# A hybrid Fourier/Hyena encoder layer: another order in the first half of its Fourier stage, xg stored by halves, a table loaded later

## The chip, the cores and the metric

The kernel runs on one core of a Trainium2 chip. The metric is the device time of one execution in microseconds, as the median of several runs; three runs of the kernel before took 2352.02, 2353.79 and 2360.07 us. One more execution was taken with the hardware profiler, and all views of the trace come from it.

## What is computed

One encoder layer is applied to two inputs of 1024 x 1024, here called batch 0 (the prompt) and batch 1 (the sample). Cut to what matters:

```
xn = rmsnorm(x, g_pre)
p  = xn @ w_in                       # 8 sections of 1024 columns
fv, fg, hv, hg, mg = split(p)
fz  = real(fft over the sequence and over groups of 256 channels of fv)
y_f = (fz * silu(fg)) @ w_fourier_out
v, x1, x2 = split(short_conv(hv))
z = v
for n, gate in enumerate((x1, x2)):
    z = gate * long_conv(z, filter[n], d[n])     # FFT convolution, length 2048
y_h = (z * silu(hg)) @ w_hyena_out
g_f, g_h = split(sigmoid(mg + b_merge))
out = (g_f * y_f + g_h * y_h) @ w_out
y = x + rmsnorm(out, g_post)
```

The filters come from a small sine network of the position, times an exponential decay, normalised per channel.

## The kernel before, in words

All products are made on TensorE (PE) with operands split into a high and a low part of fewer bits (`split`, `mm3`: high x high, high x low, low x high), so nearly every operand is rounded by ScalarE (ACT) and its remainder taken by VectorE (DVE) or GpSimd (POOL) before PE can read it. SyncE's queue (SP) issues most transfers; POOL issues some.

Four stages follow one another: the Fourier branch (`phase_fourier`, for batch 0 and then batch 1), the filters (the loop of 16 rounds in `phase_main`), the convolutions with their gates (`branches`), and the output products (`phase_tail`). Outside of marked blocks the order of each engine's instructions is set by a planner, which lays the program out with its own estimates of time; each engine then works through its list in that order, and waits at an instruction until its operands are there and the buffer it writes is free. A name with `bufs=2` has two buffers, so that the third tile of that name waits for all use of the first.

**`first_half` (lines 359 to 582)** makes the Fourier branch's first products for batch 0. Inside `with self.in_order()` the written order holds on PE, DVE, ACT and SP (not on POOL). The rows of x come in two sets, h = 0 and h = 1 (`ROWS`), of four blocks of 128 rows each, and the channels k in four pairs kp. Its steps:

- `square(h, j, eng)`: sum of squares of one block of rows, on ACT or on DVE; `norms(h)`: the factor 1/rms of the four blocks, a root on ACT and five small steps on DVE; `scale(h, n)`: four blocks times their factor, two on DVE and two on ACT, for half n of the channels.
- `trans(h, kp)`: eight transposes on PE into two PSUM tiles of the tag T (two buffers); `evac(h, kp)`: ACT moves them to the tile xg (two buffers), times g_pre, and SP stores xg to d_x.
- `fold(h, kp)`: DVE makes the sum and the difference of xg and its mirror image, eo; `high` (ACT) rounds them to eh, `rest` (DVE) takes the remainder el.
- `load_w(kp)`, `sums(kp)`, `cast(kp)`, `lows(kp)`: the weights of a pair are loaded (SP), added and subtracted (DVE), rounded (ACT), and their remainder taken (DVE). Two pairs of load buffers: `load_w(3)` waits for `sums(2)`.
- `products(h, kp, es)`: for each e in es (0 even, 1 odd), eight matmuls that read eh, then four that read el; with both e the eh matmuls of both come first, 24 in all.
- `warm(n)`: products of the identity with itself, whose result is overwritten.

A product in full f32, as of the identity or in `xtile`, makes two matmuls in the trace; a transpose makes one.

**`xtile` (lines 584 to 608)** is batch 1's counterpart, called for k = 0 to 7: load xk, eight products with a diagonal matrix in two groups of four, each moved by ACT to one half of xg, then one store of all of xg by SP, then eo, eh and el as above. Its order is the planner's, and the rest of batch 0's Fourier branch (tiles sev, sst, pp, qp, fA, fB and the stores d_fz, which POOL issues) runs among it.

**The filter rounds (lines 1178 to 1197).** In round i, `filter_taps` of round i + 1 makes the taps T (DVE, four buffers together with other tiles), `filter_spectrum` of round i transforms them and stores the result kt to d_k with three transfers a group, from two buffers. Beside them run projections (`spill_gate`, tiles wr, wh, wl, pin), for which POOL takes the low part wl. In the rounds 12, 13 and 14 the program loads a third of the table cinv each, on POOL's queue. These loads wait only for their room (which tile `sums` had before); the planner may put them anywhere behind that. The table is first read in `branches`.

Of the kernel before, what the change touches and what calls it, by code (L numbers as in the profile page):

```python
# [16 lines left out]
P = 128  # L17
D = 1024
L = 1024
# [142 lines left out]
class K:  # L162
# [196 lines left out]
    def first_half(self, pw, W, fo, px, pf, later, sine):  # L359
# [33 lines left out]
        def lows(kp):  # L393
            for i, r in enumerate((we[kp], wo[kp])):
                self.sub("dve", W[i][1][:, ks(kp)], r, W[i][0][:, ks(kp)])
# [22 lines left out]
                else:  # L418
                    nc.scalar.mul(x, x, s)

        def trans(h, kp):
            for j in range(2):
                k = 2 * kp + j
                t = tp[h, kp, j] = self.psum("T", 2, "tpx")
                for q, m in enumerate(sorted(self.ROWS[h])):
                    nc.tensor.transpose(t[:, q * P:(q + 1) * P], xs[m][:, k * P:(k + 1) * P], self.ident)

# [27 lines left out]
        def high(h, kp):  # L455
            nc.scalar.copy(part(0, h, kp), eo[h, kp].rearrange("p k e r a -> p (k e r) a"))
# [37 lines left out]
        with self.in_order():  # L494
            nc.scalar.activation(root[:, 0:1], self.ones[:, 0:1], AF.Sqrt)
            for j in range(4):
                square(0, j, "act" if j < 3 else "dve")
            norms(0)
            scale(0, 0)
            p = {}  # L500
            sumsof(0)
            sumsof(1)
            trans(0, 0)
            scale(0, 1)
            sums(0)
            load_w(2)
            evac(0, 0)
            cast(0)
            trans(0, 1)
            fold(0, 0)  # L510
            high(0, 0)
            evac(0, 1)
            lows(0)
            rest(0, 0)
            warm(14)
            products(0, 0)
            sums(1)
            cast(1)
            square(1, 0, "act")
            fold(0, 1)  # L520
            trans(0, 2)
            high(0, 1)
            evac(0, 2)
            lows(1)
            rest(0, 1)
            products(0, 1)
            square(1, 1, "act")
            square(1, 2, "dve")
            square(1, 3, "dve")
            sums(2)  # L530
            load_w(3)
            norms(1)
            scale(1, 0)
            trans(1, 0)
            fold(0, 2)
            cast(2)
            high(0, 2)
            evac(1, 0)
            trans(1, 1)
            lows(2)  # L540
            rest(0, 2)
            products(0, 2)
            fold(1, 0)
            evac(1, 1)
            sums(3)
            high(1, 0)
            cast(3)
            fold(1, 1)
            scale(1, 1)
            trans(0, 3)  # L550
            rest(1, 0)
            products(1, 0)
            evac(0, 3)
            high(1, 1)
            lows(3)
            fold(0, 3)
            trans(1, 2)
            rest(1, 1)
            products(1, 1)
            evac(1, 2)  # L560
            high(0, 3)
            fold(1, 2)
            trans(1, 3)
            rest(0, 3)
            self.opened = self.left
            products(0, 3)
            evac(1, 3)
            high(1, 2)
            fold(1, 3)
            rest(1, 2)  # L570
            products(1, 2)
            high(1, 3)
            rest(1, 3)
            r5 = fo["r5"].unsqueeze(2).to_broadcast([P, 8, 2])
            self.split(fo["x5"][:, :, 0:33:32], fo["x5"][:, :, 2:35:32], r5, "dve", "act")
            products(1, 3)
            made = self.operands(pf)
            for e in range(2):
                for m in (0, 2):
                    self.keep(made, e, m, p[e, m])  # L580
            sine()
        return made, {q: t for q, t in p.items() if q[1] % 2}

    def xtile(self, b, k, px, fo):


        nc, a = self.nc, self.a
        xt = px.tile([P, 8, P], F32, tag="x", name=f"xk{b}_{k}", bufs=3)
        nc.sync.dma_start(xt.rearrange("p m c -> p (m c)"), a["x1c"][k])
        xg = px.tile([P, L + 2], F32, tag="xg", name=f"xg{b}_{k}", bufs=2)  # L590
        nc.gpsimd.memset(xg[:, L:L + 2], 0.0)
        for n in range(2):
            tp = self.psum("mm", 4, "tpx")
            for q in range(4):
                m = 4 * n + q
                self.mm(tp[:, q * P:(q + 1) * P], xt[:, m], self.diag[:, m], True, True)
            nc.scalar.activation(xg[:, 512 * n:512 * n + 512], tp, AF.Copy, scale=self.gpre[:, k:k + 1])
        nc.sync.dma_start(self.d_x[b][k], xg[:, 0:L])
        eo = px.tile([P, 2, 2, 256], F32, tag="eo", name="eo", bufs=2)
        fw = xg[:, 0:512].rearrange("p (a r) -> p r a", r=2)  # L600
        bw = xg[:, 1024:512:-1].rearrange("p (a r) -> p r a", r=2)
        self.add("dve", eo[:, 0], fw, bw)
        self.sub("dve", eo[:, 1], fw, bw)
        self.split(fo["eh"][:, k], fo["el"][:, k], eo, "dve", "act")
        x5 = fo["x5"][:, k]
        hi = x5[:, b:b + 33:32]
        nc.scalar.copy(hi, xg[:, 512:513].to_broadcast([P, 2]))
        nc.scalar.activation(x5[:, 2 + b:35 + b:32], hi.bitcast(F32), AF.Identity, bias=xg[:, 512:513], scale=-1.0)
# [538 lines left out]
    def phase_main(self, nct=8, nb=NB, nf=16):  # L1147
        tc, nc, a = self.tc, self.nc, self.a
        with ExitStack() as es:
# [28 lines left out]
            for i in range(nf):  # L1178
                if i in (3, 5, 7, 9):
                    k = (i - 3) // 2  # L1180
                    r = room[:, 2048 * (k % 2):2048 * (k % 2) + 2048].rearrange("p (q n) -> p q n", q=4)
                    self.block_sums([r[:, q] for q in range(4)], 0, k, [self.d_x[1][k + 4 * j] for j in range(2)])
                nxt = self.filter_taps((i + 1) % 2, (i + 1) // 2, rates, ws) if i + 1 < nf else None
                self.filter_spectrum(i % 2, i // 2, taps, ws)
                if i + 2 < nf:
                    rates = self.filter_rates(i % 2, i // 2 + 1, ws, self.rounded)
                taps = nxt
                for sec, c in fill[i * len(fill) // nf:(i + 1) * len(fill) // nf]:
                    self.spill_gate(0, sec, c, ws)
                if i == 12:  # L1190
                    self.cinv = mi.tile([P, 2, INVW], F32R, tag="cinv", name="cinv", bufs=1)
                    self.cin0 = mi.tile([P, 4 * P], F32, name="cin0")
                    nc.sync.dma_start(self.cin0, a["c_in0"])
                if 12 <= i < 15:

                    s = slice((i - 12) * INVW // 3, (i - 11) * INVW // 3)
                    nc.gpsimd.dma_start(self.cinv[:, :, s], a["c_inv"][:, :, s])
            self.branches(nb, nct, ws, mi)

# [680 lines left out]
```

## Time and profile before

| what | us |
|---|---|
| median of three runs | 2353.79 |
| the profiled execution, its own time | 2355.18 |
| its span (first to last instruction) | 2353.4 |
| PE busy in the span | 2323.0 |
| DVE busy | 1973.4 |
| ACT busy | 1107.4 |
| POOL busy | 409.3 |
| cinv's three loads issued | 296.5 to 297.9 |
| first matmul that reads cinv | 718.6 |
| xtile's stores of xg, first and last issue | 102.7 to 128.5 |

All times inside the execution count from the start of its span. An engine's row in a timeline says when a run of instructions began, how long it was busy, the line of the kernel, the operation and its tiles (written <- read); a bracket behind it gives the idle time ahead and what ended it. In the rows of the windows view stand, behind the stretch and its length, the busy time of PE, PE's weight loads, DVE, ACT and POOL, then the granted clock of TensorE, the busy share of the transfer engines and GB/s.

### The profile page before, as it was taken

The page shows a single profiled execution, that of the slowest core. Times are in us where ns is not written, and L with a number is a line of the kernel's source. Part 1 is how long each engine was busy: PE and PEld are TensorE (multiplying, and loading weights), DVE is VectorE, ACT ScalarE, POOL GpSimd, SP SyncE. Part 2 cuts the span into 40 slices and gives each one's busy share as a digit, 9 for nine tenths or more (in the row PEclk, how much of TensorE's full clock was granted, in tenths as well). Part 3 has the DMA queues.
Part 4 walks back from the last instruction along what each step waited for, and adds up shares of the span by engine and source line. Part 5 has one row for each costly group of instructions (what it writes and reads, how often), then busy time and mean ns, then how long its engine had stood idle before and what let it go on. Part 6 is the DMA issues. An engine that isn't in the chain of part 4 may idle for free.

```text
span 2353.4 us, 36339 instructions
## 1 busy us (share of the span) xinstructions
PE 2323.0 (99%) x12852; PEld 2024.6 (86%) x12852; DVE 1973.4 (84%) x3479; ACT 1107.4 (47%) x2073; POOL 409.3 (17%) x386
## 2 busy tenths in 40 slices
PE   8999999999999999999999999999999999999998
PEld 7999888888888888888888888888888888888787
DVE  8775788888889999999989989997755578778987
ACT  7654566667653333334222222333443365556443
POOL 1002322322342342321000000122000000101311
PEclk9999999999999999999999999999999999999999
DMA  8636865555566667666555554445853678998654
GB/s 283 215 120 223 270 213 177 173 168 174 180 223 210 206 197 218 205 199 238 183 175 174 175 171 162 159 155 206 306 171 140 219 263 271 265 314 246 200 163 143
DMA packets 246208, 479.71 MB, mean 204 GB/s; under 512 B 24582, under 2 KB 82280, under 8 KB 245706
## 3 DMA queue, kind: packets, MB, share of 16 engines
q1 hardware_dynamic: 222013, 402.25, 51.1%
q0 software_dynamic: 23792, 75.11, 11.2%
q8 instruction: 101, 1.65, 0.3%
q14 instruction: 81, 0.66, 0.1%
q10 hardware_dynamic: 221, 0.04, 0.0%
HBM read 326.82 MB, written 177.73 MB: 214 GB/s over the span
## 4 chain that ended last, share of the span: by engine, by line
PE 56%; DVE 2%; DMA 1%; issue 1%; ACT 0%; POOL 0%; DVEq 0%; SPq 0%; POOLq 0%; ACTq 0%
PE pin L195 19%; PE pg L195 15%; PE pn L195 12%; PE pT L195 5%; PE pX L195 5%; PE tph L1065 1%; DMA xr<-in_x 0%; DMA d_m<-gt 0%; DVE wl L182 0%; DMA oB<-d_wo 0%; DVE room L182 0%; DVE wraw L182 0%; DVE o L182 0%; DVE gt L182 0%; DVE x L178 0%
## 5 line engine op out<-in xcount | busy, mean ns | idle before, releaser
L195 PE MATMUL pin<-x,wh 128*128 128x512 f32 x2816 | 889.5, 391 | 0.0
L195 PEld LDWEIGHTS pin<-x,wh 128*128 128x128 f32 x2816 | 523.4, 188 | 99.3
L195 PE MATMUL pin<-x,wl 128*128 128x512 f32 x1408 | 551.0, 391 | 0.0
L182 POOL TENSOR_TENSOR wl<-wr,wh 128x512 fp32r<-128x512 f32 x128 | 237.4, 1855 | 715.1 <-ACT wh L172 684.9
L195 PEld LDWEIGHTS pin<-x,wl 128*128 128x128 f32 x1408 | 264.9, 188 | 49.7
L195 PE MATMUL pn<-room,wh 128*128 128x512 f32 x864 | 265.9, 389 | 0.0
L195 PEld LDWEIGHTS pn<-room,wh 128*128 128x128 f32 x864 | 162.2, 188 | 33.5
L195 PE MATMUL pn<-room,wl 128*128 128x512 f32 x432 | 168.2, 389 | 0.1
L182 DVE TENSOR_TENSOR t<-pX,k 128x1024 f32<-128x1024 f32 x128 | 155.8, 1217 | 10.4 <-DMA k<-d_k 5.4
L195 PE MATMUL pX<-bh,cfwd 128*128 128x256 f32 x768 | 161.4, 289 | 0.6 <-DVE t L182 0.6
L195 PE MATMUL pT<-cinv,yh 128*128 128x256 f32 x768 | 145.4, 284 | 0.4 <-DVE T0s L182 0.4
L172 ACT CAST wh<-wr 128x512 fp32r<-128x512 f32 x128 | 79.1, 618 | 123.3 <-PE pin L195 75.0
L172 ACT CAST bh<-b 128x512 fp32r<-128x512 f32 x144 | 88.7, 619 | 93.9 <-DVE b L182 64.3
L195 PEld LDWEIGHTS pX<-bh,cfwd 128*128 128x128 f32 x768 | 126.2, 190 | 3.3 <-DVE t L182 1.2
L195 PEld LDWEIGHTS pT<-cinv,yh 128*128 128x128 f32 x768 | 122.8, 191 | 6.2 <-issue 0.6
L1521 POOL DMA_DIRECT2D d_m<-gt x32 | 27.1, 848 | 532.7 <-DVE gt L182 507.5
L172 ACT CAST yh<-y 128x512 fp32r<-128x512 f32 x96 | 59.5, 619 | 116.7 <-DVE y L182 116.7
L195 PE MATMUL pX<-bl,cfwd 128*128 128x256 f32 x384 | 109.2, 284 | 0.0
L195 PE MATMUL pT<-cinv,yl 128*128 128x256 f32 x384 | 109.0, 284 | 0.1
L182 DVE TENSOR_TENSOR bl<-b,bh 128x512 fp32r<-128x512 f32 x144 | 101.1, 706 | 3.7 <-ACT bh L172 3.6
L1066 ACT COPY xt<-tph 128x512 f32<-128x512 f32 x64 | 36.9, 587 | 130.7 <-PE tph L1065 130.5
L195 PEld LDWEIGHTS pn<-room,wl 128*128 128x128 f32 x432 | 81.1, 188 | 17.4 <-DVE wl L182 0.5
(377 smaller groups left out, 5114.4 us busy)
## 6 DMA issues: line engine op xcount, KB each, us to landing
k<-d_k SPq DMA_DIRECT2D x128, 512.0 KB, 4.2
wr<-in_w_in SPq DMA_DIRECT2D x128, 256.0 KB, 3.4
d_g<-gt SPq DMA_DIRECT2D x124, 256.0 KB, 2.6
wl<-d_s SPq DMA_DIRECT2D x56, 512.0 KB, 5.5
d_k<-kt SPq DMA_DIRECT2D x128, 128.0 KB, 2.2
d_k<-kt SPq DMA_DIRECT2D x64, 256.0 KB, 2.3
g<-d_g SPq DMA_DIRECT2D x64, 256.0 KB, 5.0
r<-d_g SPq DMA_DIRECT2D x60, 256.0 KB, 5.8
```

Source lines behind the costliest of these rows:

```text
L172: self.rounded = nc.scalar.copy(h, src)
L182: return e.tensor_tensor(out, a, b, op=op)
L195: return self.nc.tensor.matmul(out, lhsT, rhs, start=start, stop=stop, skip_group_check=shared)
L1065: nc.tensor.transpose(tp[:, q * P:(q + 1) * P], eo[:, e, q], self.ident)
L1066: nc.scalar.copy(xt[:, e].rearrange("p a b -> p (a b)"), tp)
L1521: nc.gpsimd.dma_start(dst, t, accum_op=ADD)
```

## The change

In `first_half`: `trans` gets a number of dummy products that PE makes into the tile before its first transposes, and is called with 14 for h = 1, kp = 0. The third square of set 1 goes from DVE to ACT. The factors, the scaling and the transposes of set 1 now stand ahead of `sums(2)` and `load_w(3)`. `products(0, 1)` is split: its even half stays, its odd half follows the transposes. `high(0, 2)` goes behind `evac(1, 0)` and `trans(1, 1)`. In `xtile` each half of xg is stored by its own transfer. In `phase_main` each third of cinv is preceded by a copy of one column from the newest taps to that third, by POOL, so that the load waits for this copy.

```diff
-        def trans(h, kp):
+        def trans(h, kp, fill=0):
             for j in range(2):
                 k = 2 * kp + j
                 t = tp[h, kp, j] = self.psum("T", 2, "tpx")
+                for _ in range(0 if j else fill):
+                    self.mm(t[:, 0:P], self.ident, self.ident, True, True)
                 for q, m in enumerate(sorted(self.ROWS[h])):
                     nc.tensor.transpose(t[:, q * P:(q + 1) * P], xs[m][:, k * P:(k + 1) * P], self.ident)
...
             rest(0, 1)
-            products(0, 1)
+            products(0, 1, (0,))
             square(1, 1, "act")
-            square(1, 2, "dve")
+            square(1, 2, "act")
             square(1, 3, "dve")
+            norms(1)
+            scale(1, 0)
+            trans(1, 0, 14)
+            products(0, 1, (1,))
             sums(2)
             load_w(3)
-            norms(1)
-            scale(1, 0)
-            trans(1, 0)
             fold(0, 2)
             cast(2)
-            high(0, 2)
             evac(1, 0)
             trans(1, 1)
+            high(0, 2)
             lows(2)
             rest(0, 2)
             products(0, 2)
...
-            nc.scalar.activation(xg[:, 512 * n:512 * n + 512], tp, AF.Copy, scale=self.gpre[:, k:k + 1])
-        nc.sync.dma_start(self.d_x[b][k], xg[:, 0:L])
+            s = slice(512 * n, 512 * n + 512)
+            nc.scalar.activation(xg[:, s], tp, AF.Copy, scale=self.gpre[:, k:k + 1])
+            nc.sync.dma_start(self.d_x[b][k][:, s], xg[:, s])
...
                     s = slice((i - 12) * INVW // 3, (i - 11) * INVW // 3)
+                    nc.gpsimd.tensor_copy(self.cinv[:, 0, s.start:s.start + 1], taps[0][:, 0, 0, 0, 0:1])
                     nc.gpsimd.dma_start(self.cinv[:, :, s], a["c_inv"][:, :, s])
```

## The prediction

> **What bounds the kernel now.** I read the page's busy times and its chain of work first, then the list of what TensorE (PE) waited for, and then the timelines around those waits.
>
> ```profile
> PE 2323.0 (99%) x12852; PEld 2024.6 (86%) x12852; DVE 1973.4 (84%) x3479; ACT 1107.4 (47%) x2073; POOL 409.3 (17%) x386
> PE pin L195 19%; PE pg L195 15%; PE pn L195 12%; PE pT L195 5%; PE pX L195 5%; PE tph L1065 1%; DMA xr<-in_x 0%; DMA d_m<-gt 0%; DVE wl L182 0%; DMA oB<-d_wo 0%; DVE room L182 0%; DVE wraw L182 0%; DVE o L182 0%; DVE gt L182 0%; DVE x L178 0%
> ...
> PE tpx L426 <- issue: 3.2, 1, 3.2
> PE pse L195 <- ACT sev L698: 2.5, 1, 2.5
> PE pXf L195 <- ACT kt L972: 1.9, 1, 1.9
> PE pXf L195 <- DVE b L182: 1.8, 1, 1.8
> ```
>
> The reader should see that PE is busy for 2323.0 us of the span, and that the chain that ends last is nearly all matmuls. So an edit can win only what PE stands idle, 2353.4 - 2323.0 = 30.4 us in all, or runs slowly, and whatever PE gains early it keeps unless another engine catches it. The edits lie around three of the waits: 3.2 us in the first half of the Fourier stage (edits of `first_half`), 2.5 us in the second batch's transposes (xg by halves), and 1.8 us in the third filter round (late table). The wait of 1.9 us, one round ahead of that, is not touched. The granted clock in these places:
>
> ```profile
> 34.00:36.00 2.00, 1.35 (x7) 1.35 (x8) 1.97 (x3) 1.66 (x6) 0.00 (x0) 0.50 0.67 153
> 116.00:118.00 2.00, 2.00 (x12) 2.00 (x11) 1.97 (x4) 1.25 (x4) 0.10 (x1) 0.52 1.00 322
> 300.00:320.00 20.00, 18.02 (x94) 15.01 (x93) 16.58 (x34) 10.58 (x24) 3.20 (x2) 1.00 0.87 282
> ```
>
> Behind the idle times of 3.2 and 2.5 us PE runs at a granted clock of 0.50 to 0.52; behind the one of 1.8 us (it lies between 300 and 320) it stays at 1.00. In this trace the clock falls somewhere between 1.8 and 2.5 us of idleness.
>
> **Change, part one: first_half.** All engines but POOL keep the written order there, so I carry the rows forward in the new order.
>
> ```profile
> 17.38 3.29 PE L195 MATMUL pfv<-ident 128*128 128x128 f32 x28
> 24.83 1.23 DVE L182 TENSOR_TENSOR el<-eo,eh 128x1024 fp32r<-128x1024 f32 x1 [0.45 <-ACT eh L456]
> 25.97 1.22 DVE L402 CUSTOM_DVE_ANT_0 el<-x 128x1024 fp32r<-128x1024 f32 x1
> 26.09 1.06 ACT L400 ACTIVATE eh<-x 128x1024 fp32r<-128x1024 f32 x1
> 27.05 0.19 ACT L400 ACTIVATION_READ_ACCUMULATOR eh<-x 128x1 f32 x1
> 28.39 0.43 DVE L182 TENSOR_TENSOR wes<-wfv 128x260 f32<-128x260 f32 x1
> 29.81 0.17 DVE L408 RECIPROCAL rs<-root 128x4 f32<-128x4 f32 x1
> 30.60 0.88 DVE L417 TENSOR_SCALAR x<-x,rs 128x512 f32<-128x512 f32 x2
> 31.40 1.29 DVE L182 TENSOR_TENSOR eo<-xg 128x512 f32<-128x512 f32 x2
> 32.88 1.04 ACT L456 CAST eh<-eo 128x1024 fp32r<-128x1024 f32 x1
> 33.92 1.25 ACT L435 ACTIVATE xg<-tpx,gpre 128x512 f32<-128x512 f32 x2
> 33.95 1.22 DVE L182 TENSOR_TENSOR el<-eo,eh 128x1024 fp32r<-128x1024 f32 x1
> 36.27 1.80 PE L195 MATMUL pfv<-we,eh 128*128 128x260 f32 x8
> 39.77 1.21 DVE L182 TENSOR_TENSOR el<-eo,eh 128x1024 fp32r<-128x1024 f32 x1
> 42.60 0.64 PE L195 MATMUL pfv<-we,el 128*128 128x260 f32 x4
> ```
>
> *Removed from VectorE (DVE):* one square of 1.22 us, which becomes one of ScalarE (ACT), 1.06 + 0.19 = 1.25 us there. ACT now ends its second square at 26.09 + 2 x 1.25 = 28.6, whereas DVE, done with its only square at 27.2, must wait for it. Root to scaling takes about 1.15 us (0.3 for the root, 30.60 - 29.81 = 0.79 behind it), so scaling starts at 29.75 instead of 30.60. The third weights' sums, moved behind it, take about 1.35 us (29.81 - 28.39, less 0.07 for the step of the norm between them): scaling 0.80 (31.40 - 30.60), then sums, put `fold(0, 2)` at 31.9 instead of 31.40. So the square that DVE loses comes back as waiting, and it is 0.5 us late here.
>
> *Moved on ACT:* `high(0, 2)` (1.04 us) goes behind `evac(1, 0)` (1.25 us). ACT's casts wait for the late sums and end at 32.8 (two steps of some 0.55 us behind the last even sum at 31.65), the eviction ends at 34.1, the copy at 34.2, `high(0, 2)` at 35.25. DVE's `rest(0, 2)` needs it, so it starts at 35.27 and not at 33.95: 1.3 us late, with nothing else in DVE's order to fill the hole. From there DVE has in before hardly any idle time (1.97 of 2.00 us busy in the row of 34 to 36) up to `rest(1, 0)` at 39.77; the same steps (5.8 us) put that at 41.07 and its end at 42.3.
>
> *Added on PE:* 14 dummy products. Row 17.38 shows that 14 calls make 28 matmuls in 3.29 us. They begin when `products(0, 1, (0,))` ends (24.85 + 12 x 0.12, its last four behind el at 26.06: 26.7) and end at 30.0; the transposes can begin at 29.75 + 0.43 + 0.1 = 30.3. So the dummies fit the hole and cost nothing; were the scaling 0.3 us earlier than I think, they would begin to hold the transposes up. The held-back 12 products (1.45 us) follow the transposes, from 31.9 to 33.35, while ACT evicts: hidden as well. Thus PE doesn't idle 3.2 us and should keep the clock.
>
> *The sum on PE:* `products(0, 2)` can start at 35.3 (before: 36.27, at half clock). It ends some 1.55 us ahead, and `products(1, 0)` comes 1.6 us ahead to its low terms, which read what `rest(1, 0)` writes. That is ready at 42.3; before, the row 42.60 is this very matmul. So of 1.6 us only **0.3 us** is left, and PE shows a new wait of about 1.3 us for DVE at 41 us. After that DVE (without a hole up to 45.5) and PE run level. SP's third and fourth weights' loads (two issues) wait for the sums, 2.7 us later than now; they are read from 37.6 on, over 5 us behind, which hides a load of 260 KB; a later landing would widen DVE's hole, and the upper bound holds that. Bounds: -1.6 (DVE's hole doesn't form) to +1.0 (the hole grows by another eviction's 1.25 us). I take -0.3, the row-by-row sum.
>
> **Part two: xg by halves.** Each of the eight rounds stores xg with two transfers of 256 KB, the first behind the first eviction.
>
> ```profile
> 102.90 0.69 ACT L597 ACTIVATE xg<-tpx,gpre 128x512 f32<-128x512 f32 x1
> 105.80 0.53 POOL L752 DMA_DIRECT2D d_fz<-fA  x1 [10.28 <-DVE fA L178]
> 106.13 0.33 SPq L598 DMA_DIRECT2D d_x<-xg  x1
> 113.06 0.69 ACT L597 ACTIVATE xg<-tpx,gpre 128x512 f32<-128x512 f32 x1 [2.77 <-DMA d_x<-xg]
> 116.64 3.31 PE L195 MATMUL tpx<-dg,xk 128*128 128x128 f32 x16
> 120.89 1.95 PE L195 MATMUL tpx<-dg,xk 128*128 128x128 f32 x16
> ...
> 110.00:112.00 2.00, 1.98 (x18) 1.81 (x17) 2.00 (x5) 0.30 (x1) 0.00 (x0) 1.00 1.03 412
> 120.00:122.00 2.00, 2.00 (x20) 2.00 (x19) 1.86 (x4) 1.97 (x5) 0.00 (x0) 1.00 0.52 102
> ```
>
> ACT stands 2.77 us at 113.06 for the store issued at 106.13: with two buffers, the fourth round's eviction needs the second round's store. ACT's queue holds behind it a cast and the copy sev, for which PE waits the 2.5 us of the list. The store took 6.9 us because stores of d_fz went out beside it (from 105.80) and the transfer engines were full, 1.03 at 412 GB/s. After the change half of it leaves at 103.6, ahead of them. The other half still leaves at 106.13, with 256 KB less ahead in its own queue and, if both queues get equal shares, 256 KB less of the other's in between: 0.52 MB at 412 GB/s, 1.3 us. PE's idleness goes to 1.2 us, below the 1.8 that left the clock alone; 16 transposing matmuls then take 1.95 and not 3.31 us, up to 1.4 us more. But ACT is nearly full behind it (1.97 of 2.00 us at 120 to 122), so PE may meet it again; I count half of the 1.4. Together **-2.0 us**. SP's eight more issues cost 0.33 us each and stand ahead of loads for which PE waits nowhere in this stage; uncovered, eight of them are 2.6 us. Bounds: -3.9 (2.5 + 1.4) to +1.0 (a load pushed late, three issues' worth).
>
> [...]
>
> **Part three: late table.** The three parts of cinv leave POOL's queue now as soon as their room is free.
>
> ```profile
> cinv<-in_c_inv POOLq DMA_DIRECT2D x3, 768.0 KB, 10.2
> d_k<-kt SPq DMA_DIRECT2D x6, 128.0 KB, 9.0
> d_k<-kt SPq DMA_DIRECT2D x128, 128.0 KB, 2.2
> ...
> 309.99 1.00 DVE L178 SCALAR_TENSOR_TENSOR kt<-pXf,th,ktmp 128x256 f32<-128x256 f32 x3 [3.42 <-DMA d_k<-kt]
> 593.29 2.38 POOL L182 TENSOR_TENSOR wl<-wr,wh 128x512 fp32r<-128x512 f32 x1 [8.19 <-ACT wh L172]
> L924 PE MATMUL pn<-acc,ones x32: 270/272/275, 264.2 to 665.7; 128*128 128x128 f32 x32
> 650.00:680.00 30.00, 30.00 (x164) 26.00 (x164) 28.18 (x62) 15.65 (x34) 13.56 (x12) 1.00 0.71 226
> ```
>
> They are 3 x 768 KB, and between 296 and 312 us the small stores of d_k take 9.0 us to land, over the whole program 2.2. DVE waits 3.42 us for a kt buffer at 309.99, and PE then the list's 1.8 us for DVE's b. Without the burst DVE is up to 3.4 us earlier, so PE's **1.8 us** go entirely. The copies that now precede the transfers read the taps of rounds 13, 14 and 15; the matmuls of L924 close the taps, two rows in each of sixteen rounds, from 264.2 to 665.7, so a round is (665.7 - 264.2) / 15 = 26.8 us and the parts move to about 605, 635 and 660 us. There PE waits for nothing and the transfer engines are 0.71 full; 768 KB at 412 GB/s is 1.9 us of them each time. Cost between 0 and 1.8 (what the whole burst does now); I take **+0.3**, a sixth of that, as each part is a third of the burst and DVE has there 1.8 of 30 us free. The copy itself is three instructions on POOL, idle there for 8.19 us ahead of a row such as 593.29.
>
> **Sum.** -0.3 - 2.0 - 1.8 + 0.3 = -3.8 us. The span goes to 2349.6, the profiled execution from 2355.18 to 2351.4. That execution lies 1.4 above the median of the runs, 2353.79; on the median the forecast is **2350.0 us**, 0.16% less.
>
> [...]
>
> **Rivals.**
> *All gaps close, faster:* DVE's hole doesn't form (-1.6), the second gap goes with all its slow clock (-3.9), the table gives 1.8 and costs nothing: -7.3, 2346.5 us. For it: PE has no other bound in those rows. Against: ACT and DVE are full behind both gaps.
> *Less from the halves:* of the store that waits only its own bytes count, 256 KB at 412 GB/s or 0.6 us, the gap stays at 1.9 and the clock as it is: -0.6 for -2.0, so -2.4 in all, 2351.4 us. For it: the second half still leaves at 106.13. Against: the 6.9 us of a transfer that needs 1.3 at that rate.
> *No change:* the store stays late because the engines are at 412 GB/s whichever way it is cut, first_half gives nothing, and the three parts delay d_k stores late as they do early, against the 1.8 won: about 0, 2353.8 us; with a part of one gain 2352 to 2354.
> *Slower:* POOL works in order, and the copies wait for DVE's taps. If the planner puts a copy half a round (26.8 / 2 = 13.4 us) ahead of its taps, the weights' low parts wl stand behind it. POOL's idleness of 8.19 us covers the first part; the remaining 5.2 us hold PE's pin products up, three times: +15.6 - 4.1 (the gains) = +11.5, 2365.3 us. It decides from a wait of 8.2 us on. Against it: the copy needs only the first quarter of the taps, and today's rows show wl waiting for ACT, not the other way.
>
> **Chances.** Forecast 0.43, less from the halves 0.14, no change 0.20, all gaps close 0.17, slower 0.06. Differences under 0.3% (7.1 us) can't be told from no change here; only the case in which all gaps close passes it downward, if just, and the slower one upward: faster 0.17, same 0.77, slower 0.06. The range leaves out the slower case and about the lower half of the fastest one; upward, the bounds of parts one and two (+1.0 and +1.0) beside a table that gives nothing make 2355.8. So it is 2345.5 to 2355.5.
>
> **What would show it.** Right: no PE wait for L426 at 28 to 31 us, a granted clock of 1.00 from 30 to 40, a new PE wait of about 1.3 us for DVE's el near 41, DVE idle for 1 to 1.5 us twice between 27 and 36; PE's wait for sev about 1.2 and the clock at 1.00 behind it; no PE wait for b at 314, d_k stores landing in under 4 us there. Wrong: a clock under 1.00 at 30 to 40, dummies that end behind the scaling, ACT still waiting over 2 us for d_x, POOL waiting over 8 us in front of a copy, or new waits of pin for wl after 590. A changed planned order elsewhere could move more than any of these terms.

## The result: 0.13% less time, and the profile after

| | changed kernel | before, same chips |
|---|---|---|
| median, us (20 runs each) | 2351.64 (2347.66 to 2355.42) | 2354.53 (2350.56 to 2360.07) |
| ratio, 95% interval | 0.9987 (0.9981 to 0.9993) | |
| the profiled execution | 2352.65 | 2355.18 |
| its span | 2350.8 | 2353.4 |

That is 2.9 us less (1.6 to 4.5 by the interval), where 3.8 were forecast: a difference smaller than the 0.3% under which the prediction counted a time as unchanged. The sum came out nearly right, by luck: two of its three terms did not. The busy times from the page of the changed kernel:

```profile
PE 2326.5 (99%) x12880; PEld 2027.2 (86%) x12880; DVE 1971.9 (84%) x3477; ACT 1108.7 (47%) x2075; POOL 411.2 (17%) x389
```

PE's busy time includes the 3.29 us of new dummies, and the span is shorter all the same: PE stands idle 2350.8 - 2326.5 = 24.3 us, against 30.4 before. What it still waited for, from the list of PE's waits (sum, times, longest; one of 3.8 us for the filter's weights, 3.7 before, is left out):

```profile
PE tpx L428 <- DVE x L417: 2.1, 2, 1.6
PE tpx L195 <- DMA xk<-in_x1c: 1.7, 1, 1.7
PE pn L195 <- DVE wl L182: 1.4, 2, 1.1
PE pfv L195 <- DVE el L182: 1.0, 1, 1.0
PE pXf L195 <- ACT kt L976: 0.9, 1, 0.9
PE pse L195 <- ACT sev L702: 0.7, 1, 0.7
```

All three waits that the prediction aimed at are gone or small: 3.2 (transposes) is 0.5 in its place (1.6 of the 2.1 come earlier, in the first loads), 2.5 (sev) is 0.7, 1.8 (b) is not in the list. New are 1.7 for xk, 1.0 for el and 1.4 for wl. The granted clock (the third number from the end of a row) in the places shown of before:

```profile
34.00:36.00 2.00, 1.88 (x15) 1.45 (x14) 1.78 (x3) 1.97 (x6) 0.63 (x2) 1.00 0.83 305
116.00:118.00 2.00, 2.00 (x19) 2.00 (x20) 1.36 (x3) 1.19 (x3) 0.10 (x1) 1.00 1.04 405
300.00:320.00 20.00, 20.00 (x103) 17.08 (x102) 18.72 (x42) 15.05 (x36) 3.24 (x3) 1.00 0.52 164
```

**Lead.** To see where time comes from, I took each matmul's start in the profile of before less its start in another kernel's profile (same tile, same occurrence), and the median of this over a stretch: how far that kernel is ahead. The row 42.60 quoted of before, for example, starts at 43.64 here: it is 1.04 us behind. The table gives the lead at 20 us and what it grew by in each stretch, for every profile of this study, and the last column the sum, the lead at 2250.

| kernel | at 20 | to 46 | to 85 | to 150 | to 320 | to 2000 | to 2250 | lead |
|---|---|---|---|---|---|---|---|---|
| changed kernel | -2.17 | 1.03 | 1.86 | 0.18 | 3.49 | 0.67 | -2.53 | 2.53 |
| the same again (e11) | 0.17 | 0.45 | 1.67 | -0.31 | 2.66 | -0.06 | -1.13 | 3.45 |
| first half alone (e1) | -1.66 | 1.04 | 1.86 | 0.29 | 3.30 | 0.24 | -1.05 | 4.02 |
| halves alone (e2) | -2.60 | 1.92 | 0.41 | 0.51 | -1.79 | 1.59 | -1.07 | -1.03 |
| late table alone (e3) | -0.04 | -0.20 | 0.40 | 1.06 | 2.45 | -0.21 | -2.37 | 1.10 |
| all but halves (e4) | 0.91 | 0.45 | 1.86 | -0.16 | -0.35 | 1.02 | -0.87 | 2.85 |
| before + delay (e5) | -0.63 | 0.29 | -2.21 | 0.51 | -1.56 | -6.06 | -0.72 | -10.37 |
| no dummies (e6) | -1.09 | 1.04 | -0.08 | 0.64 | 2.59 | -0.66 | -2.07 | 0.37 |
| square on DVE (e7) | 0.10 | 0.33 | 1.06 | -0.10 | 3.10 | 0.19 | -0.65 | 4.03 |
| high first (e8) | 0.93 | 1.07 | 1.34 | -0.18 | 4.28 | 0.81 | -0.87 | 7.38 |
| late burst (e9) | -1.29 | 1.04 | 1.81 | -1.85 | 4.00 | -0.03 | -1.75 | 1.93 |
| halves by POOL (e10) | -2.06 | 1.04 | 0.93 | -1.57 | 4.15 | 0.04 | -2.98 | -0.46 |
| high first, whole (e12) | -1.83 | 1.69 | 1.38 | 0.91 | 4.33 | 0.78 | -0.97 | 6.30 |

One execution stands behind each row. The same kernel twice (rows one and two) differs by 2.3 us at the start and by 1.4 in the last stretch, and by up to 0.9 in each stretch between. That is not the most that chance does: e5 has the order of the kernel before on every engine up to 326 us, and yet its lead falls by 2.21 to 85 us and by 1.56 from 150 to 320. In both stretches its clock was halved for 3.41 us (at 79.5 us, where two products took 0.78 us for 0.51 in before, and at 318.4, with 0.50 from 319 to 321), where that of before was not. So a single growth of 1 to 2 us in this table proves nothing by itself; it counts where many profiles agree, or where the waits behind it are shown. A kernel that starts late also catches up by itself (e2 by 1.92 to 46 us, with no edit there): that column is read among equal starts.

### The profile page after: what moved, and what is told of

Read it like the earlier page. It is cut to its first block, busy times and chain, and to the rows that moved or that the text cites. A ratio compares the mean times of both kernels' runs of the same rounds, so it can differ in the third digit from the quotient of the medians.

```text
span 2350.8 us, 36414 instructions
## 1 busy us (share of the span) xinstructions
PE 2326.5 (99%) x12880; PEld 2027.2 (86%) x12880; DVE 1971.9 (84%) x3477; ACT 1108.7 (47%) x2075; POOL 411.2 (17%) x389
## 4 chain that ended last, share of the span: by engine, by line
PE 55%; DVE 2%; DMA 2%; issue 1%; ACT 0%; POOL 0%; DVEq 0%; SPq 0%; POOLq 0%; ACTq 0%
PE pin L195 19%; PE pg L195 16%; PE pn L195 9%; PE pT L195 5%; PE pX L195 5%; PE tph L1069 1%; DMA d_m<-gt 1%; DMA wraw<-d_m 1%; DMA g<-d_g 0%; DVE wl L182 0%; DVE r L182 0%; DVE gt L182 0%; DVE room L182 0%; DMA wl<-d_s 0%; DVE x L178 0%
## 5 line engine op out<-in xcount | busy, mean ns | idle before, releaser
L182 POOL TENSOR_TENSOR wl<-wr,wh 128x512 fp32r<-128x512 f32 x128 | 231.0, 1805 | 700.4 <-ACT wh L172 669.5
```

The source lines that it names most:

```text
L182: return e.tensor_tensor(out, a, b, op=op)
```

## The experiments

Each time is a median beside the kernel before on the same chip. The ratio is taken from all runs and not from the two medians, and can differ from theirs (e6: 0.9986 by the medians).

| kernel | us (runs) | before | ratio, 95% interval |
|---|---|---|---|
| e1 first half alone | 2350.18 (11) | 2353.57 | 0.9985 (0.9976 to 0.9993) |
| e2 halves alone | 2354.86 (12) | 2353.57 | 1.0001 (0.9991 to 1.0010) |
| e3 late table alone | 2351.88 (11) | 2353.57 | 0.9989 (0.9980 to 0.9997) |
| e4 all but halves | 2351.47 (11) | 2353.57 | 0.9984 (0.9975 to 0.9993) |
| e5 before + delay | 2362.22 (5) | 2354.85 | 1.0035 (1.0022 to 1.0048) |
| e6 no dummies | 2351.67 (11) | 2354.85 | 0.9995 (0.9986 to 1.0004) |
| e8 high first | 2349.66 (11) | 2354.85 | 0.9978 (0.9970 to 0.9987) |
| e10 halves by POOL | 2351.36 (11) | 2354.85 | 0.9992 (0.9983 to 1.0001) |
| e7 square on DVE | 2350.81 (11) | 2354.05 | 0.9985 (0.9976 to 0.9994) |
| e9 late burst | 2351.04 (11) | 2354.05 | 0.9987 (0.9978 to 0.9996) |
| e11 changed again | 2350.24 (11) | 2354.05 | 0.9983 (0.9974 to 0.9992) |
| e12 high first, whole | 2349.20 (10) | 2354.05 | 0.9982 (0.9973 to 0.9991) |

### The three parts alone, and the change without one (e1 to e4)

e1 is the kernel before with the edits of `first_half` only, e2 with the halves only, e3 with the table's copy only; e4 is the changed kernel with xg stored whole:

```diff
-            s = slice(512 * n, 512 * n + 512)
-            nc.scalar.activation(xg[:, s], tp, AF.Copy, scale=self.gpre[:, k:k + 1])
-            nc.sync.dma_start(self.d_x[b][k][:, s], xg[:, s])
+            nc.scalar.activation(xg[:, 512 * n:512 * n + 512], tp, AF.Copy, scale=self.gpre[:, k:k + 1])
+        nc.sync.dma_start(self.d_x[b][k], xg[:, 0:L])
```

e1 has this and, as the kernel before, no copy ahead of the table's loads:

```diff
-                    nc.gpsimd.tensor_copy(self.cinv[:, 0, s.start:s.start + 1], taps[0][:, 0, 0, 0, 0:1])
```

e3 is the kernel before with that line added, e2 the kernel before with the first diff the other way round.

> Only the edits of first_half. Theory 1 (the parts add up as forecast): 0.3 us faster at the end; at 46 us PE is 0.3 to 1.0 us ahead of the kernel before, apart from what the start differs, with a PE wait of about 1 us for el near 42. Theory 2 (a later place paced by transfers levels it): the same lead at 46 us, but between 75 and 85 us PE's wait for ee in front of x loads grows by what was won, so at 90 us nothing is left: 0.0 +- 0.5 us.

> Only xg by halves. Theory 1 (as forecast): PE's wait for sev falls from 2.5 to about 1.2 us, the clock stays at 1.00, 2.0 us ahead at 140 us. Theory 2 (the wait changes its place): the wait for sev falls, but PE waits 1 to 2 us for an xk load, because SP's queue holds xk behind more stores: between 0 and 0.7 us ahead at 140 us.

> Only the late table. Theory 1 (the burst of cinv at 296 us made both waits of the filter rounds longer): no PE wait for b at 314 us, 2 to 3.5 us ahead at 340 us, and no loss up to 720 us. Theory 2 (half of the 3.5 us seen there came from the earlier parts, which shifted the phase): 1.8 us ahead at 340 us, with the wait of 1.9 us for kt at 297 as it was. At the end: 3 us faster if nothing gives it back, 0 to 1.5 if the output stage does.

> The changed kernel with xg stored whole again. If the halves are worth 2.0 us as forecast, this is 2 us slower than the changed kernel (about 2353.6 beside 2351.6); if the wait only changed its place, the same within 0.5 us, with PE's wait for sev and the low clock at 116 us back and no wait for xk.

The first half alone gained 2353.57 - 2350.18 = 3.4 us, over ten times its forecast; the halves nothing (1.3 us more by the medians, and a ratio of 1.0001); the table 1.7 us by the medians and 2.6 by the ratio, beside its 1.5. Whether the parts add up the runs leave open: by the ratios the first and the third make 3.5 + 2.6 = 6.1 us and both together 3.8 (e4), but each of the three is uncertain by some 2 us.

The traces show one place where they could overlap. PE's wait for b near 314 us, 1.8 us in before, is 2.1 in e2 and 2.3 in e5, which keep the table's burst too, and it is gone in every kernel with the late table; but it is gone in e1 as well, which keeps the burst (the section on the late table has the rows). Between 150 and 320 us e1 gains 3.30, e3 2.45, and the changed kernel, with both, 3.49 and 2.66 in its two profiles. If e1 lost that wait in every execution, the two parts would remove the same wait, and together remove it once; there is one profile of e1. (e4's -0.35 there goes with a wait of 3.08 us for kt in that one execution, behind which the clock was halved: 0.72 from 298 to 302.) What became of the halves, and whether a gain is given back later, the next runs ask.

### Where the halves went (e10)

The halves did what they should: PE's wait for sev fell from 2.5 to 0.7, and to 0.8 in e2. But PE now waits for xk, 1.7 us in the changed kernel and 1.3 in e2. Two issues of xk in the timeline of before, then the timeline of the changed kernel there:

```profile
107.14 1.81 SPq L589 DMA_DIRECT2D xk<-in_x1c  x1
110.38 1.06 SPq L589 DMA_DIRECT2D xk<-in_x1c  x1
```

```profile
105.35 2.79 SPq L602 DMA_DIRECT2D d_x<-xg  x2
107.10 0.69 ACT L601 ACTIVATE xg<-tpx,gpre 128x512 f32<-128x512 f32 x1 [1.78 <-DMA d_x<-xg]
108.24 0.38 SPq L592 DMA_DIRECT2D xk<-in_x1c  x1
108.81 2.91 SPq L602 DMA_DIRECT2D d_x<-xg  x2
111.81 1.30 SPq L592 DMA_DIRECT2D xk<-in_x1c  x1
113.20 0.99 PE L195 MATMUL pse<-seq,oo 128*128 128x258 f32 x6 [0.71 <-ACT sev L702]
115.89 2.02 PE L195 MATMUL tpx<-dg,xk 128*128 128x128 f32 x16 [1.70 <-DMA xk<-in_x1c]
```

SP's list goes out in order in these rows. A half's store waits at SP for its own eviction, and that one for an older store, so two stores hold SP for 2.79 and 2.91 us; the loads xk behind them go out at 108.24 and 111.81, where they went out at 107.14 and 110.38 before, although this kernel is 0.8 us ahead here. Then PE waits 1.70 us for xk. Nor is the clock safe: in the second profile of the same kernel (e11) it was halved at 113.84 all the same (0.69 from 116 to 118). In e10 POOL issues the half stores:

```diff
-            nc.sync.dma_start(self.d_x[b][k][:, s], xg[:, s])
+            nc.gpsimd.dma_start(self.d_x[b][k][:, s], xg[:, s])
```

> The changed kernel with the half stores of xg issued by POOL instead of SP. Theory one, SP's queue: a half store that waits for its eviction holds SP, so the loads xk behind it are issued 1.1 to 1.4 us later than before (108.24 and 111.81 for 107.14 and 110.38), and PE waits 1.7 us for xk. With the stores off SP the xk issues go back by over 1 us, PE's wait for xk falls under 0.5 us, its wait for sev stays near 0.7, and the lead over the kernel before grows by 1 to 1.7 us between 100 and 140 us: 2350.0 to 2350.6 where the changed kernel takes 2351.6. Theory two, full transfer engines: xk lands late whoever issues the stores (4.7 to 7.5 us after its issue), PE still waits 1 us or more for xk, and the time is that of the changed kernel within 0.7. Theory three: POOL now holds the d_fz stores behind waiting xg stores, ACT or DVE waits for fA's buffers, and the stage loses more than it gains (over 2352.5).

```profile
102.04 10.49 SPq L592 DMA_DIRECT2D xk<-in_x1c  x5
106.76 0.54 POOL L756 DMA_DIRECT2D d_fz<-fA  x1 [0.41 <-issue]
107.81 0.54 POOL L602 DMA_DIRECT2D d_x<-xg  x1
115.92 1.26 ACT L601 ACTIVATE xg<-tpx,gpre 128x512 f32<-128x512 f32 x2 [3.93 <-DMA d_x<-xg]
116.66 2.08 PE L195 MATMUL tpx<-dg,xk 128*128 128x128 f32 x8 [3.05 <-ACT xg L601]
```

In this timeline of e10 the five loads xk follow one another from 102.04 on, and PE has no wait for xk in its list. That alone would not decide, since PE now stands for xg in the same place; the landings do. The load that PE waited for in the changed kernel was issued at 108.24 and landed at 115.75. In e10 it was issued at 107.17 and landed at 113.69, and PE came there at 116.66 - 3.05 = 113.61. So SP's queue was the reason for most of that wait; the transfer itself takes 6.5 us here and 7.5 there, which leaves it little room. But now the half stores stand on POOL behind d_fz's (106.76), ACT waits 3.93 us for d_x and PE 3.05 us for xg. The wait has changed its queue a second time; the stretch to 150 us lost 1.57. So theory one names the cause, theory three is right that POOL's order costs as much (though it is d_x that stands behind d_fz), and its time, 2351.36, shows no gain.

The table of leads says the same of the halves over many profiles: from 85 to 150 us the seven with half stores on SP grow by -1.85 to 0.64 (mean -0.2), the five besides before with whole stores by -0.16 to 1.06 (mean 0.5).

### The first half: dummies, square, high (e6, e7, e8)

Three edits of the changed kernel, each in a kernel of its own. e6:

```diff
-            trans(1, 0, 14)
+            trans(1, 0)
```

> The changed kernel without the 14 dummy products in front of set 1's first transposes. Theory one, the clock: PE idles about 3.3 us ahead of the transposes, the granted clock falls to 0.5 for 3.4 to 6.8 us behind it, and the lead at 42 to 54 us is 0.5 to 1.5 us less than the changed kernel's (compared from the lead that each has at 24). Theory two, DVE sets the time: the products that follow wait for DVE's el in any case (1.0 us at 42.6), the slow clock eats that wait and no more, and the lead at 42 to 54 is the same within 0.4; then the time of the whole is that of the changed kernel, 2351.6, within 0.7.

e7:

```diff
-            square(1, 2, "act")
+            square(1, 2, "dve")
```

> The changed kernel with the square of set 1's third block back on DVE. Theory one, as in the prediction's row-by-row sum: what DVE saves by giving the square away comes back as a wait of 1.2 us for ACT's square, so with the square back DVE has no such wait, its norm starts within 0.2 us of where it did, and the lead at 42 to 54 us, from the same lead at 24, is the changed kernel's within 0.3. Theory two, DVE is the bound from here to 45 us and each of its microseconds counts: the lead there is 1.0 to 1.2 us smaller, and PE's wait for el grows from 1.04 to over 2 us.

e8:

```diff
+            high(0, 2)
             evac(1, 0)
             trans(1, 1)
-            high(0, 2)
```

> The changed kernel with high(0, 2) back ahead of evac(1, 0) and trans(1, 1). Theory one: DVE's hole of 0.9 us ahead of rest(0, 2) comes from ACT's eviction standing first; with the cast first rest(0, 2) starts 1.2 us sooner, rest(1, 0) ends about 1 us sooner, PE's wait of 1.04 us for el near 42.6 goes, and the lead at 46 to 54 us is 0.7 to 1.0 us larger than the changed kernel's, from the same lead at 24. Theory two: the eviction is then 1.04 us later, fold(1, 0) waits for it in the hole's place, rest(1, 0) ends where it did within 0.3 us, and the lead at 46 to 54 is the same within 0.3.

The changed kernel's timeline beside which these are read, with the steps that the prediction dated:

```profile
27.86 3.29 PE L195 MATMUL tpx<-ident 128*128 128x128 f32 x28
29.99 0.17 DVE L407 TENSOR_SCALAR low<-ss 128x4 f32<-128x4 f32 x1 [3.40 <-ACT eh L400]
31.67 0.56 PE L428 MATMUL tpx<-ident,x 128*128 128x128 f32 x2 [0.53 <-DVE x L417]
36.66 1.23 DVE L182 TENSOR_TENSOR el<-eo,eh 128x1024 fp32r<-128x1024 f32 x1 [0.89 <-ACT eh L458]
43.64 0.75 PE L195 MATMUL pfv<-we,el 128*128 128x260 f32 x4 [1.04 <-DVE el L182]
```

It is 2.17 us behind at 20 us, but the order of events is the forecast's: the dummies fill the hole, the norm waits for ACT's square (3.40 us here, 1.25 in e11, which starts level; 1.4 forecast), DVE has a hole of 0.89 ahead of el, and PE a new wait of 1.04 for el (1.3 forecast).

e6, from its timeline and its windows:

```profile
30.62 2.34 PE L428 MATMUL tpx<-ident,x 128*128 128x128 f32 x8 [3.67 <-issue]
50.23 0.19 ACT L434 COPY xg<-r 128x2 f32<-128x2 f32 x1 [3.54 <-DMA d_x<-xg]
52.81 1.22 PE L195 MATMUL pfv<-we,eh 128*128 128x260 f32 x8 [1.57 <-ACT eh L458]
```

```profile
34.00:36.00 2.00, 2.00 (x12) 2.00 (x11) 1.11 (x3) 1.60 (x4) 0.53 (x1) 0.50 0.82 232
```

Without the dummies PE idles 3.67 us and the clock is at 0.50 behind it, yet the lead grows to 46 us by 1.04, as in e9, which has the dummies and a like start (1.04): theory two. Eight transposes at half clock (2.34 us) take what PE would have waited for el. Its later loss, 1.57 us at 52.81, comes from a store of xg for which ACT waits 3.54 us; the same wait of ACT's is 1.69 us in e9 and 1.55 in e11, and no run here ties it to the dummies. By the times it can't be told from the changed kernel. e7's DVE makes both squares and starts its norm with no wait (two rows of its timeline):

```profile
28.44 0.17 DVE L407 TENSOR_SCALAR low<-ss 128x4 f32<-128x4 f32 x1
42.07 0.75 PE L195 MATMUL pfv<-we,el 128*128 128x260 f32 x4 [1.04 <-DVE el L182]
```

Its lead grows by 0.33 to 46 us, and e11's (which starts level as well) by 0.45; PE's wait for el is 1.04 in both. So giving the square away buys nothing: theory one. e8 against e4, which starts with the same lead (0.93 and 0.91); from the timelines, first e4's rows, then e8's:

```profile
34.18 1.23 DVE L182 TENSOR_TENSOR el<-eo,eh 128x1024 fp32r<-128x1024 f32 x1 [0.89 <-ACT eh L458]
41.15 0.75 PE L195 MATMUL pfv<-we,el 128*128 128x260 f32 x4 [1.04 <-DVE el L182]
```

```profile
33.20 1.22 DVE L182 TENSOR_TENSOR el<-eo,eh 128x1024 fp32r<-128x1024 f32 x1
33.88 1.23 PE L428 MATMUL tpx<-ident,x 128*128 128x128 f32 x8 [1.56 <-ACT xg L437]
```

With the cast first el starts 0.98 us sooner, and PE's 1.04 us at el are gone. PE waits 1.56 us for xg at its transposes instead, which costs less than it seems, as products follow that have nothing else to wait for: the lead grows by 1.07 to 46 us against 0.45, 0.6 more. e12, behind a late start, grows by 1.69 against 1.03 to 1.04. So theory one, with 0.6 of the 0.7 to 1.0 expected.

### Is a delay carried to the end, and does the last stage level gains? (e5, e11)

e5 puts 28 more products into the filter stage of the kernel before:

```diff
+            for _ in range(28 if (n, ct, m) == (0, 4, 0) else 0):
+                self.mm(ps[:, 0:P], self.ident, self.ident, True, True)
```

> The kernel before with 28 dummy products more (56 matmuls, about 6.5 us of PE) in the filter stage, at the taps' first round. Theory one, PE is the bound to the end: all of the delay is carried on, within 1 us, to the last instruction, and the time is 6 to 7 us more than the kernel before, about 2360. Theory two, the output stage is set by its transfers (the engines are about 1.0 busy from 2010 to 2200): whatever PE loses early is made up in part there, as what it won was given back in part there (2.5 of 5.1 us in the changed kernel), so between 2050 and 2240 the lag shrinks by 1.5 us or more and the time is 3 to 5 us more than the kernel before.

> The changed kernel once more, on the chip of the next three runs, for two questions. In its first profile DVE waited 6.99 us for the load of wraw near 2174, and PE then 0.72 us for gt and 1.07 us for wl; a kernel with the same order on PE there (high(0, 2) put back ahead) waited 4.42 us and PE not at all. Theory one, the landing of that load varies from execution to execution: the second profile has another wait there (under 5 us, or over 6 again by chance), and the same order gives lags that differ by over 1.5 us between 2150 and 2200. Theory two, it follows from this kernel's order: the waits of 0.7 and 1.07 recur within 0.3 us. Its time, beside those of the other three here, is what they are compared with: 2351 to 2352.

e5's lead falls by 6.06 between 320 and 2000 and by 0.72 more to 2250, no less than other kernels there; its time is 7.4 us longer. So PE is the bound to the end, and nothing is levelled: theory one. What the changed kernel lost at the end (2.53) is another thing. Its timeline, then that of the same kernel in e11:

```profile
2174.37 0.69 DVE L182 TENSOR_TENSOR wsum<-wraw 128x512 f32<-128x512 f32 x1 [6.99 <-DMA wraw<-d_m]
2176.53 0.70 PE L195 MATMUL pn<-room,wh 128*128 128x512 f32 x2 [0.72 <-DVE gt L182]
2178.30 0.50 PE L195 MATMUL pn<-room,wl 128*128 128x512 f32 x1 [1.07 <-DVE wl L182]
```

```profile
2171.82 0.69 DVE L182 TENSOR_TENSOR wsum<-wraw 128x512 f32<-128x512 f32 x1 [4.92 <-DMA wraw<-d_m]
```

The same program waits 6.99 us for the load of wraw in one execution and 4.92 in the other, where PE waits for gt not at all: theory one. The five profiles in which that wait is over 6 us (changed, e3, e6, e9, e10) lose 1.75 to 2.98 in the last stretch, the eight others 0.65 to 1.13. All five have the late table, but so have five of the others (e4, e7, e8, e11, e12); whether the late table makes the long wait more likely, these profiles don't tell.

### The late table (e9)

```diff
-                if 12 <= i < 15:
+                if i == 12:
...
+                    for j in range(3):
+                        s = slice(j * INVW // 3, (j + 1) * INVW // 3)
```

> The changed kernel with all three thirds of cinv behind the first of the late copies, near 591 us, as one burst of 2.3 MB there. Theory one, a burst costs only where small stores with two buffers are waited for at the same time and PE has no slack: near 591 us the d_k stores land late (over 5 us), but PE waits for nothing, and the time is the changed kernel's within 0.7. Theory two, the burst costs what it cost at 296 us wherever it stands: PE waits 1.5 to 2 us for wl, b or kt between 590 and 625 us, and the time is 1.5 to 2 us above the changed kernel's on this chip.

The transfers issued between 585 and 605 us in e9 (KB each, median us to landing):

```profile
cinv<-in_c_inv POOLq DMA_DIRECT2D x3, 768.0 KB, 8.5
d_k<-kt SPq DMA_DIRECT2D x4, 128.0 KB, 4.0
```

The d_k stores take 4.0 us to land beside the burst, not over 5, and PE waits for nothing between 560 and 700 us. The time is 0.8 us above that of the changed kernel on this chip, which the runs can't tell from nothing. Theory two is out: the burst doesn't cost there what it cost at 296 us. The late landings of theory one did not come either, so PE's slack was not put to the test. Of the transfers issued between 290 and 320 us, e3's row of d_k:

```profile
d_k<-kt SPq DMA_DIRECT2D x10, 128.0 KB, 2.7
```

With the burst gone d_k lands in 2.7 us, from 296 to 312 as well, where before took 9.0, and DVE's wait of 3.42 us for kt is not there. In e2 and e5, which keep the burst, PE's wait for b was 2.1 and 2.3 us, the clock was halved behind it (0.70 from 314 to 318 in e2, 0.50 from 319 to 321 in e5), and the lead fell by 1.79 and 1.56: of these three profiles that of before, with 1.8 us and no halving, shows the burst at its cheapest.

e1 still has the burst, but DVE waits only 1.07 us. Its order from 99 to 318 us is that of before on every engine; only the times differ. From the timelines, the burst and the kt stores in before, then the same in e1 with the row of DVE that has the wait:

```profile
296.45 2.20 POOL L1197 DMA_DIRECT2D cinv<-in_c_inv  x3 [0.28 <-DMA d_k<-kt]
298.01 0.98 SPq L977 DMA_DIRECT2D d_k<-kt  x2
```

```profile
294.52 2.21 POOL L1200 DMA_DIRECT2D cinv<-in_c_inv  x3 [0.99 <-DVE kt L178]
295.37 1.28 SPq L980 DMA_DIRECT2D d_k<-kt  x2
305.14 1.00 DVE L178 SCALAR_TENSOR_TENSOR kt<-pXf,th,ktmp 128x256 f32<-128x256 f32 x3 [1.07 <-DMA d_k<-kt]
```

With two buffers DVE waits for the stores of the kt before last, and by the times its wait ends with the landing of the second of these two. In before that store was issued at 298.46, behind the third part of the table (297.94), and landed at 309.87, just behind that part (309.65). In e2 and e5 it was the same: issued 0.5 us behind the third part, landed 0.2 us behind it, 11.8 and 11.9 us after its issue. In e1 it was issued at 295.96, just ahead of the third part (296.01), and landed at 305.01, while that part landed at 307.33. So in these four profiles the wait goes with which of the two queues issued first, POOL with the third part or SP with the store, and that is a matter of half a microsecond. Whether e1's edits bring that about in every execution, or one execution had it by chance, is not shown.

### High first with whole stores (e12)

e8's edit and e4's together.

> high(0, 2) back ahead of evac(1, 0), and xg stored whole; the late table and the rest of the first half's edits as in the changed kernel. Theory one, the halves are worth nothing (0 +- 1 by the run of them alone): the time is that of the kernel with high(0, 2) first and halves, 2349.7, within 0.7, and some 2 us under the changed kernel on this chip. Theory two, as forecast the halves are worth 2 us: about 2351.7, no better than the changed kernel. In the trace the lead over the kernel before at 46 to 54 us is by 0.5 to 0.7 larger than that of the changed kernel with whole stores (from the same lead at 24), since PE's wait of 1.04 for el is gone.

It has the lowest median of all, 2349.20, and is 1.0 us under the changed kernel on the same chip; by the ratios (0.9982 and 0.9983) that is not told apart. Against e8 (0.9978) nothing that the runs can tell is lost by storing xg whole: theory one, the halves are worth nothing.

## Why the prediction was right in sum and wrong in its terms

**What bounds the kernel: right.** PE is the bound, and a delay put in behind 326 us is still there at 2250 us (e5).

**Part one, -0.3: right where it looked, too small in all.** From a start that was not late the lead to 46 us grew by 0.45 (e4, e11). The square came back as waiting (e7), DVE had its hole (e8), the dummies fitted, though they were worth nothing up to 46 us (e6). What failed is the limit of the sum: it ended at 46 us ("After that DVE (without a hole up to 45.5) and PE run level"). One more wait went further on: in before, e2, e3 and e5 PE waits 0.5 to 1.1 us for ee at 78 us, and in none of the nine kernels with the first half's edits: their leads grow by 0.93 to 1.86 from 46 to 85 us (e6 aside, with its loss at 52.81), the others' by 0.41 at most. The wait is up to 1.1 us of that; what makes up the rest was not traced. From the timelines, PE's row and SP's issues in before, then SP's in the changed kernel:

```profile
78.46 0.51 PE L195 MATMUL pfv<-we,eh 128*128 128x260 f32 x2 [1.14 <-DVE ee L182]
71.87 1.37 SPq L338 DMA_DIRECT2D x<-in_x  x2
73.33 1.84 SPq L619 DMA_DIRECT2D wfv<-in_w_fv  x2
```

```profile
73.39 0.33 SPq L338 DMA_DIRECT2D x<-in_x  x1
74.11 0.33 SPq L623 DMA_DIRECT2D wfv<-in_w_fv  x1
74.49 0.42 SPq L338 DMA_DIRECT2D x<-in_x  x1
```

The planner, which starts from what `first_half` leaves behind, now issues the loads of x and of the weights in turn, and the order of DVE's work differs too; which of the two removes the wait was not tried. This is the "changed planned order elsewhere" that the prediction named, and it was larger than the term. The rest of e1's gain lies near 300 us, where its order is that of before, and stays open as said above.

**Part two, -2.0: wrong.** The failed step is "SP's eight more issues cost 0.33 us each and stand ahead of loads for which PE waits nowhere in this stage". PE doesn't wait for xk while sev holds it up for 2.5 us (before); it does, for 1.7, as soon as sev takes 0.7 (the changed kernel). And an issue that waits for its eviction holds the queue as long as that takes, up to 2.9 us for two. Of the terms, the wait of 2.5 fell by 1.8, and xk gave 1.7 of it back; the clock, of which 0.7 us were counted, stayed up in the first profile and was halved in the second. Issued between 98 and 116 us, the stores of xg of 512 KB landed in 4.3 us (median) in before, and those of 256 KB in 5.3 in the changed kernel.

**Part three, -1.8 + 0.3: the mechanism right.** Without the burst neither DVE's 3.42 nor PE's 1.8 us appears (e3), alone it is worth 1.7 us by the medians, and of the 0.3 for a late cost no trace shows anything: PE waits nowhere between 560 and 700 us, not even for the whole burst (e9). The parts went out at 592, 617 and 651 us, where 605, 635 and 660 were forecast. POOL's copies did wait for taps, and one took 5.17 us itself (the timeline of the changed kernel), yet no wl came late: the slower rival's place was right, and its wait, 6.10 us, stayed below the 8.2 from which it was to decide.

```profile
615.95 0.31 POOL L1201 CAST cinv<-T 128x1 fp32r<-128x1 f32 x1 [6.10 <-DVE T L182]
645.11 5.17 POOL L1201 CAST cinv<-T 128x1 fp32r<-128x1 f32 x1
```

What the step missed is that the wait also goes without it, when the stores leave ahead of the burst's third part (e1); in such an execution parts one and three count it once.

**The sum:** -3.8 forecast, -2.9 measured (-3.8 in e11): part one's surplus stands in for part two. That is luck, not a sum that held. **The chances:** the time is within 0.3%, the likeliest of the three.

**The clock:** "somewhere between 1.8 and 2.5 us of idleness" was not a threshold at all. Behind a wait for sev of 2.54 us the clock stayed up in e1 (sixteen products tpx in 1.95 us, and 1.00 from 116 to 118), and behind one of 1.88 it was halved in e12 (sixteen in 3.04 us, and 0.74 from 116 to 118).

## What to carry over

When a wait on one engine is removed, look first at the queue that its buffer's other users share: here two issues that waited for their operands held the later loads of SP's queue for 2.79 and 2.91 us, and their price was that wait and not the 0.33 us of an issue. Two edits can act on the same wait, so measure the parts alone as well as together, and each in more than one profile: here programs of the same order differed by 2.2 us within one stretch. Where a planner lays out what follows, an edit's effect behind its own stretch can be larger than in it; compare start times of the same matmuls before explaining a total.

## What the runs showed of the chip

**The stretches at half clock are 3.41 or 6.83 us long.** Ahead of the program's end, the granted clock was 0.50 from 30.76 to 37.59 and from 116.09 to 119.51 us in before, and from 14.98 to 21.80 and from 2179.03 to 2182.44 in the changed kernel. In rows of 1 us it was so for 6.8 us in e5 (from 31.7), in e6 (from 30.0) and in e10 (from 116.0), and for 3.4 us in e5 (from 318.4) and in e8 (from 112.6). The two starts lie 85.33 us apart in before and 2164.05 in the changed kernel, which is 25 and 634 times 3.413. Counted in steps of 3.413 us from these starts, PE stood idle for 2.77, 2.47, 1.98 and 1.79 us in the steps just ahead of the four stretches of these two traces, and for 1.70 at most in the steps that no halving followed. PE's wait of 1.78 us for b in before, behind which the clock stayed up, lies in two such steps, with 1.00 and 0.97 us of idle time. The second half of the 6.83 us stands behind a step with only 1.21 us in before and 0.76 in the changed kernel, which this count doesn't explain. The length of a wait alone doesn't separate the runs: behind 2.54 us in e1 and 1.87 in e3 the sixteen products tpx took 1.95 us, behind 2.56 in e4 and 1.88 in e12 they took 3.10 and 3.04. How these four waits lie to such steps is not shown.

**The start varies.** At 20 us eight of the 14 profiles are 0.63 to 2.60 us behind that of before, the others 0.04 at most (the table of leads). In the changed kernel, e5, e6 and e10, which are among them, a stretch at half clock lies between 14 and 22 us; in before and e8, which starts 0.93 ahead, none does. The changed kernel was 2.17 us behind in one profile and 0.17 ahead in the other.
